# Prompt q, k and v in products of 512 columns, with one buffer for evictions and another opening order

## The chip, the cores and the metric

The kernel runs on one core of a Trainium2 chip. The core's engines run side by side and wait for each other through semaphores: TensorE (PE in the profile, with the loads of its stationary operand as PEld), VectorE (DVE), ScalarE (ACT), GpSimd (POOL) and SyncE (SP), which here issues nearly all transfers, in the order of its own queue. The metric is the device time of one execution in microseconds (us), median of several runs.

## The reference, cut to what matters

One encoder layer is applied to a prompt of 1024 tokens and to a sample of 512 tokens, with a model width of 1024. Everything is float32.

```python
def encoder_layer(x, ...):
    h = rmsnorm(x, norm_g)
    z = h @ w_in
    hy_in, hy_gate, att_qkv, att_gate = jnp.split(z, [3*HY_W, 4*HY_W, 4*HY_W + 3*ATT_W], axis=-1)
    ...                                  # Hyena branch: short and long convolution
    q, k, v = jnp.split(att_qkv, 3, axis=-1)                 # 512 columns each, 8 heads of 64
    q = rmsnorm(q.reshape(B, L, N_HEADS, HEAD_DIM), qn_g)
    k = rmsnorm(k.reshape(B, L, N_HEADS, HEAD_DIM), kn_g)
    y_att = neighbourhood_attention(q, k, v, rpb)
    y_att = rmsnorm(y_att, on_att) * jax.nn.silu(att_gate)
    return x + jnp.concatenate([y_hy, y_att], axis=-1) @ w_out
```

The Hyena branch's filter is a small network (mlp) of sines on positions, with two layers and a third product w3, multiplied by a decay; its spectrum K is multiplied with that of the branch's input.

## The kernel before

A float32 product is made of three products of a high and a low part: hi x whi, hi x wlo, lo x whi. The parts of the normalised, transposed input are hThi_p and hTlo_p, one tile for each segment of 512 prompt tokens, with 8 pieces of 128 channels (KC = 8). A weight key is loaded by SP into wraw and split into two units, whi by a cast on ScalarE and wlo by a subtraction, mostly on GpSimd (`issue_w`); `take_w` hands the units out and keeps up to `w_bufs` = 4 of them ready.

**Opening.** `x_norm` loads and scales four x tiles of a segment, `x_turn` transposes them on TensorE (L246) and makes hThi on ScalarE and hTlo on VectorE. `mlp_seg` is one layer of the filter's mlp for 512 positions: a product (L168), steps on VectorE (arg, n: L76 to L82) and a sine on ScalarE. VectorE's order is written out by hand in `run` (manual_schedule): segment 0's x and hTlo, all of segment 1's x and hTlo, the first mlp layer, then the splitting of w3 (w3lof, w3lob) and of the transform constants (fc, dftm). Behind that a scheduler sets the order by priorities and its own estimate of times.

**First phase.** `weave` merges two chains: the filter phase (`k_phase`: products with w3 (L562, L563), a product with the decay `dec` on VectorE giving xk, sums and differences into zc and bt tiles, transforms (L453 to L455, L468) and ScalarE's copies Kw), and the projections: v, two blocks of the attention gate, then k and q. `proj_tok` makes 256 columns of v, k or q for all 1024 tokens in one pass: h is stationary, the weights move, four banks of PSUM hold two token tiles of 256 columns each, and the weights of a pass (four units) are used up in it. v, k and q take two passes each, so there are six passes of 192 products of 128x256 at L414. The gates come from `proj_ch` (L401), where the weights are stationary and 512 tokens move.

**Evictions.** Each bank of v is cast into a tile `vg` (ScalarE, L855), its remainder is subtracted (VectorE, recorded at the helper's L64) and four stores of 160 KB bring vg to DRAM (v_p). A gate's SiLU (L872) goes into a tile of the same name. There are `nvg` = 2 buffers for `vg`, and as many for `qsq`, the squares of q and k. In the filter phase dec has 3 buffers, zc 4 (`nz`), bt 3 (`nb`).

## Time and profile before

| | us |
|---|---|
| median of 3 runs | 1055.24 |
| lowest and highest run | 1054.57, 1055.99 |
| profiled execution, its own time | 1052.45 |
| span of the profiled execution | 1050.7 |
| TensorE busy | 991.8 |
| VectorE busy | 777.4 |
| ScalarE busy | 454.4 |
| GpSimd busy | 395.0 |

The rows further below come from the profiled execution. Their times count from the start of its span; what its own time has beyond the span lies around it. The first v product starts at 18.93 us, the first gate product at 92.95, the first product of k at 120.49, and the first Hyena product at 269.41. An engine that is busy for most of the span need not be the one that decides in each stage, so the rows are read by stage.

### The profile page before, as it was taken

What the parts mean: (1) busy time and instruction counts of PE and PEld (TensorE: products, weight loads), DVE (VectorE), ACT (ScalarE), POOL (GpSimd) and SP (SyncE); (2) the same over time, 40 slices, a digit from 0 to 9 for tenths busy, and PEclk for the clock granted to TensorE, in tenths of its full rate; (3) what the DMA queues carried; (4) which work ended last, traced back from release to release, by engine and by line L of the source; (5) the groups of instructions that cost most, each with busy time, mean ns of one, the idle gap of its engine ahead of it and who ended that gap; (6) DMA issues with size and microseconds to landing.
All of it is one profiled execution on the core that took longest, in us unless ns stands there. A gap on an engine that the chain in (4) does not pass through costs nothing.

```text
span 1050.7 us, 16730 instructions
## 1 busy us (share of the span) xinstructions
PE 991.8 (94%) x5868; PEld 873.1 (83%) x5868; DVE 777.4 (74%) x2039; ACT 454.4 (43%) x942; POOL 395.0 (38%) x315
## 2 busy tenths in 40 slices
PE   5889999999999999999998999998999989999998
PEld 3779799899888888888887887888988877878776
DVE  4795949654368776868558999989887877757675
ACT  7333334423331323221215565565766653456441
POOL 0012212342342322424156533435354355664540
PEclk9989999999999999999999999999999999999999
DMA  7146661653422121211393333644644469644432
GB/s 290 61 157 208 212 215 56 221 182 123 134 88 83 45 68 51 88 39 68 133 300 110 110 111 107 178 130 133 195 138 128 125 215 324 171 144 129 148 108 107
DMA packets 105491, 147.95 MB, mean 141 GB/s; under 512 B 7633, under 2 KB 69915, under 8 KB 104895
## 3 DMA queue, kind: packets, MB, share of 16 engines
q1 hardware_dynamic: 105176, 146.44, 44.6%
q8 instruction: 47, 0.77, 0.3%
q10 hardware_dynamic: 231, 0.44, 0.2%
q14 instruction: 37, 0.30, 0.1%
HBM read 105.89 MB, written 40.96 MB: 140 GB/s over the span
## 4 chain that ended last, share of the span: by engine, by line
PE 60%; DVE 20%; DMA 10%; ACT 4%; issue 3%; SPq 2%; POOL 1%; DVEq 0%; ACTq 0%; POOLq 0%
PE bank L401 26%; PE bank L414 8%; PE bank L1108 8%; PE bank L453 4%; PE bank L1022 2%; PE bank L1013 2%; PE bank L454 2%; PE bank L455 2%; DVE zc L64 2%; SPq L61 2%; DVE whi L374 1%; DVE s_sb L991 1%; DMA lo<-A_p 1%; DVE bt L64 1%; DVE s L64 1%
## 5 line engine op out<-in xcount | busy, mean ns | idle before, releaser
L64 POOL TENSOR_TENSOR wlo<-wraw,whi 128x512 fp32r<-128x512 f32 x148 | 225.5, 1529 | 474.4 <-ACT whi L374 325.7
L401 PE MATMUL bank<-hThi_p,whi 128*128 128x512 f32 x320 | 126.1, 394 | 0.8 <-DVE vg L64 0.8
L401 PE MATMUL bank<-hThi_p,wlo 128*128 128x512 f32 x320 | 126.2, 394 | 0.0
L401 PE MATMUL bank<-hTlo_p,whi 128*128 128x512 f32 x320 | 125.6, 392 | 0.0
L414 PE MATMUL bank<-whi,hThi_p 128*128 128x256 f32 x384 | 111.4, 293 | 0.8 <-ACT hThi_p L248 0.8
L414 PE MATMUL bank<-wlo,hThi_p 128*128 128x256 f32 x384 | 111.5, 291 | 0.0
L414 PE MATMUL bank<-whi,hTlo_p 128*128 128x256 f32 x384 | 110.3, 291 | 0.0
L995 ACT ACTIVATE s_sb<-s_sb,mx 128x360 f32<-128x360 f32 (+1 forms) x96 | 60.4, 630 | 83.7 <-DVE mx L991 82.8
L374 ACT CAST whi<-wraw 128x512 fp32r<-128x512 f32 x66 | 40.7, 621 | 99.6 <-PE bank L401 69.7
L1108 PE MATMUL bank<-whi,hi 128*128 128x512 f32 x192 | 76.9, 402 | 1.8 <-DVE acc L76 1.1
L1108 PE MATMUL bank<-wlo,hi 128*128 128x512 f32 x192 | 77.0, 401 | 0.0
L414 PEld LDWEIGHTS bank<-whi,hThi_p 128*128 128x128 f32 x384 | 74.9, 196 | 2.2 <-ACT hThi_p L248 1.2
L414 PEld LDWEIGHTS bank<-wlo,hThi_p 128*128 128x128 f32 x384 | 75.2, 196 | 1.2 <-issue 1.0
L1108 PE MATMUL bank<-whi,lo 128*128 128x512 f32 x192 | 75.7, 399 | 0.0
L414 PEld LDWEIGHTS bank<-whi,hTlo_p 128*128 128x128 f32 x384 | 74.4, 195 | 0.5 <-issue 0.5
L401 PEld LDWEIGHTS bank<-hThi_p,whi 128*128 128x128 f32 x320 | 60.2, 188 | 12.8 <-DVE vg L64 1.2
L1022 PE MATMUL bank<-pt,V 120*64 120x256 f32 (+1 forms) x352 | 67.2, 297 | 3.2 <-DVE pt L64 2.3
L401 PEld LDWEIGHTS bank<-hTlo_p,whi 128*128 128x128 f32 x320 | 60.2, 188 | 11.9
L401 PEld LDWEIGHTS bank<-hThi_p,wlo 128*128 128x128 f32 x320 | 60.2, 188 | 11.8
L64 POOL TENSOR_TENSOR T<-cmask,qkr 128x480 f32<-128x480 f32 x32 | 39.6, 1244 | 78.8 <-DMA qkr<-in_rpb_dram 64.3
L401 PE MATMUL bank<-hThi_s,whi 128*128 128x512 f32 x160 | 64.1, 404 | 3.4 <-ACT vg L835 3.1
L401 PE MATMUL bank<-hTlo_s,whi 128*128 128x512 f32 x160 | 63.4, 400 | 0.0
(278 smaller groups left out, 2663.6 us busy)
## 6 DMA issues: line engine op xcount, KB each, us to landing
wraw<-in_w_ch_dram SPq DMA_DIRECT2D x40, 512.0 KB
wraw<-in_w_tk_dram SPq DMA_DIRECT2D x24, 512.0 KB
V<-v_p SPq DMA_DIRECT2D x32, 240.0 KB
wraw<-in_w_out_dram SPq DMA_DIRECT2D x24, 256.0 KB
out_dram<-acc SPq DMA_DIRECT2D x24, 256.0 KB
v_p<-vg SPq DMA_DIRECT2D x32, 160.0 KB
K_p<-Kw SPq DMA_DIRECT2D x4, 1088.0 KB
x<-in_x_prompt_dram SPq DMA_DIRECT2D x8, 512.0 KB
```

The lines of the kernel that those rows point to most:

```text
L61: eng.dma_start(out=out, in_=in_)
L64: (eng or self.nc.vector).tensor_tensor(out=out, in0=a, in1=b, op=op)
L374: next(self.w_round)(out=hi, in_=r)
L401: nc.tensor.matmul(ps, lhsT=w, rhs=h[s][:, k], start=(k == 0 and i == 0), stop=(k == KC - 1 and i == 2))
L414: nc.tensor.matmul(pss[t // 2][:, t % 2, :], lhsT=h[t // 4][:, k, t % 4 * P:(t % 4 + 1) * P], rhs=w, start=(k == 0 and i == 0 and t % 2 == ...
L453: mm(o, lhsT=c, rhs=z, start=True, stop=False)
L454: mm(o[:, 0:P], lhsT=ns if inverse else s, rhs=z[:, 1], start=False, stop=False)
L455: mm(o[:, P:], lhsT=s if inverse else ns, rhs=z[:, 0], start=False, stop=True)
L995: nc.scalar.activation(out=s_sb[:, :n], in_=s_sb[:, :n], func=AF.Exp, bias=mx, scale=-1.0, accum_out=l)
L1013: nc.tensor.transpose(out=tp_[0:120, c * P:(c + 1) * P], in_=s_sb[:, c * 120:(c + 1) * 120], identity=self.ident)
L1022: nc.tensor.matmul(o, lhsT=vl, rhs=pr_, start=(c == 0 and i == 0), stop=(c == ncu - 1 and i == 1))
L1108: nc.tensor.matmul(ps, lhsT=a, rhs=w, start=(k == 0 and i == 0), stop=(k == 3 and i == 2))
```

## The change

The prompt's v, k and q come from a new function, `proj_wide`: products of 512 columns, for one segment of 512 tokens (four token tiles, one PSUM bank each). Pass 0 takes eight weight units, whi and wlo, and holds them for pass 1, so the weights are still loaded once. Six passes of 96 products of 128x512 take the place of six of 192 products of 128x256. The eight held units need eight buffers: four are in a new pool `w1`, which is closed after the first phase. A wide key is loaded by two transfers of 128x2x256. v's layout in DRAM becomes one tensor for each half, with rows of all 8 heads, and its prompt stores are 40x1024.

The filter and store buffers of the first phase become fewer: `nvg` 2 to 1, zc 4 to 3, bt 3 to 1, dec 3 to 2, and the mlp's n 2 to 1. The raw tile of the sample's q and k has one buffer where it had two. The evictions of q and k move into a helper, `qk_norm`.

In the opening, VectorE's order is another: segment 1's scaling stands between the last hTlo of segment 0, the first mlp layer's steps between the hTlo of segment 1, and each segment of the second mlp layer ahead of the splits of w3, fc and dftm.

```diff
+    def proj_wide(self, G, base, s, held):
+        pss = [self.bank(next(self.mm_tags)) for _ in range(4)]
+        for k in range(KC):
+            if not s:
+                held.append(self.take_w(("w_wide", base, k // 2)))
+            whi, wlo = held[k]
+            for t in range(4):
+                for i, (w, h) in enumerate(((whi, G.hi), (wlo, G.hi), (whi, G.lo))):
+                    self.nc.tensor.matmul(pss[t], lhsT=h[s][:, k, t * P:(t + 1) * P], rhs=w,
+                                          start=(k == 0 and i == 0), stop=(k == KC - 1 and i == 2))
...
+            pool = self.w1 if key[0] == "w_wide" and key[2] % 2 else next(self.w_pools)
...
-                decs.append(fp.tile([P, 2, 256], F32, name="dec", bufs=3))
+                decs.append(fp.tile([P, 2, 256], F32, name="dec", bufs=2))
...
+            if G is self.P_:
+                held = []
+                for s in range(G.nseg):
+                    raw = self.qk_norm(tp, self.proj_wide(G, base, s, held), 1)
...
+            pss = self.proj_wide(G, 4, gi, held) if big else self.proj_tok(4 + gi, G.hi, G.lo, G.nt)
...
+                        if big:
+                            self.dma(dst[:, gi * 4 + m].rearrange("x h d -> x (h d)"), src.rearrange("p h d -> p (h d)"))
...
-            list(self.mlp_seg(Gp, mp, 0, 1))
-            list(self.mlp_seg(Gs, mp, 0, 0))
+            turn = self.x_turn(Gp, 1, hp1)
+            next(turn)
+            next(turn)
+            for G, sg in ((Gp, 1), (Gs, 0)):
+                for _ in itertools.zip_longest(self.mlp_seg(G, mp, 0, sg), itertools.islice(turn, 3)):
+                    pass
+            a = self.mlp_seg(Gp, mp, 1, 0)
+            next(a)
             self.w3_load(mp)
+            list(a)
...
-        self.nz, self.nZ, self.nb, self.nraw = 4, 3, 3, 2
-        self.nvg = 2
+        self.nz, self.nZ, self.nb, self.nraw = 3, 3, 1, 2
+        self.nvg = 1
```

Three places show how the order of instructions moves. First VectorE in the opening, before the change, from the last hTlo of segment 0 to the first of segment 1:

```order
L76 SCALAR_TENSOR_TENSOR hTlo_p_234<-bank_284,pc_70,hThi_p_233 128x512
...
L80 TENSOR_SCALAR x_293<-x_293,rs_y4_310 128x1024
L80 TENSOR_SCALAR x_297<-x_297,rs_y4_310 128x1024
L80 TENSOR_SCALAR x_301<-x_301,rs_y4_310 128x1024
L80 TENSOR_SCALAR x_305<-x_305,rs_y4_310 128x1024
L64 TENSOR_TENSOR wlo_333<-wraw_223,whi_332 128x512
L64 TENSOR_TENSOR wlo_337<-wraw_223,whi_336 128x512
L76 SCALAR_TENSOR_TENSOR hTlo_p_341<-bank_342,pc_70,hThi_p_340 128x512
```

The same place after the change:

```order
L76 SCALAR_TENSOR_TENSOR hTlo_p_235<-bank_299,pc_70,hThi_p_234 128x512
L80 TENSOR_SCALAR x_245<-x_245,rs_y4_285 128x1024
L76 SCALAR_TENSOR_TENSOR hTlo_p_235<-bank_307,pc_70,hThi_p_234 128x512
L80 TENSOR_SCALAR x_249<-x_249,rs_y4_285 128x1024
L76 SCALAR_TENSOR_TENSOR hTlo_p_235<-bank_315,pc_70,hThi_p_234 128x512
L80 TENSOR_SCALAR x_253<-x_253,rs_y4_285 128x1024
L76 SCALAR_TENSOR_TENSOR hTlo_p_235<-bank_323,pc_70,hThi_p_234 128x512
L80 TENSOR_SCALAR x_257<-x_257,rs_y4_285 128x1024
L64 TENSOR_TENSOR wlo_335<-wraw_223,whi_334 128x512
```

The root steps for segment 1 (rs_h4, rs_y4, rs_t4) stood where the dots are and now stand ahead of the piece; the four scalings moved from behind the last hTlo to between the last four.

Then SP's queue in the gate stage, before the change, where vg_1168 and vg_1175 hold the first evicted banks of the second v pass:

```order
L61 DMA dec_564<-in_dec_p_dram 128x512
L61 DMA v_p10_99<-vg_1168 40x2x512 x2
L61 DMA dec_572<-in_dec_p_dram 128x512
L61 DMA hyb_849<-in_hy_bias_dram 1x128
L61 DMA v_p11_100<-vg_1168 40x2x512
L61 DMA dec_580<-in_dec_p_dram 128x512
L61 DMA hT0_75<-px_522 128x4x128
L61 DMA dec_588<-in_dec_p_dram 128x512
L61 DMA hyb_1248<-in_hy_bias_dram 1x128
L61 DMA hT1_76<-px_522 128x4x128
L61 DMA v_p11_100<-vg_1168 40x2x512
L61 DMA v_p10_99<-vg_1175 40x2x512
```

The same place after the change, where vg_1001 and vg_1008 hold them:

```order
L61 DMA v_p0_97<-vg_1001 40x1024 x2
L61 DMA v_p1_98<-vg_1001 40x1024
L61 DMA wraw_699<-in_w_tk_dram 128x2x256
L61 DMA dec_545<-in_dec_p_dram 128x512
L61 DMA dec_547<-in_dec_p_dram 128x512
L61 DMA hyb_549<-in_hy_bias_dram 1x128
L61 DMA wraw_699<-in_w_tk_dram 128x2x256
L61 DMA wraw_734<-in_w_tk_dram 128x2x256 x2
L61 DMA dec_558<-in_dec_p_dram 128x512
L61 DMA v_p1_98<-vg_1001 40x1024
...
L61 DMA v_p0_97<-vg_1008 40x1024 x2
```

The first dec loads, which stood ahead of these stores, now stand between them, with two weight keys, and the stores of vg_1008 come a whole eviction later.

Last, ScalarE in the gate stage, before the change, from the third eviction to the gates' SiLU (bank_1307 is the first gate product's bank):

```order
L855 CAST vg_1182<-bank_954 128x8x64
L374 CAST whi_1468<-wraw_1297 128x512
L260 ACTIVATE hl_1229,pss_1228<-px_1226 128x1024
L855 CAST vg_1189<-bank_955 128x8x64
L374 CAST whi_1472<-wraw_1297 128x512
L872 ACT_TABLE_LOAD
L872 ACTIVATE vg_1357<-bank_1307 128x512
```

The same place after the change (bank_1141 is the first gate product's bank):

```order
L895 CAST vg_1015<-bank_903 128x8x64
L895 CAST vg_1022<-bank_904 128x8x64
L386 CAST whi_1487<-wraw_1300 128x512
L386 CAST whi_1491<-wraw_1300 128x512
L386 CAST whi_1303<-wraw_1130 128x512
L917 ACT_TABLE_LOAD
L917 ACTIVATE vg_1191<-bank_1141 128x512
```

The order of the evictions and the SiLU is the same, but the tiles named vg now share one buffer, and the weight casts that stand between are of other keys.

## Rows read from the trace of the kernel before

**Rows 1.** The profile's page: PE's busy time, and the chain's shares by engine.

```profile
PE 991.8 (94%) x5868; PEld 873.1 (83%) x5868; DVE 777.4 (74%) x2039; ACT 454.4 (43%) x942; POOL 395.0 (38%) x315
PE 60%; DVE 20%; DMA 10%; ACT 4%; issue 3%; SPq 2%; POOL 1%; DVEq 0%; ACTq 0%; POOLq 0%
```

**Rows 2.** Windows: length, busy time by engine, PE's clock share, DMA share, GB/s.

```profile
18.00:31.00 13.00, 10.55 (x71) 10.14 (x70) 6.47 (x11) 9.79 (x18) 0.00 (x0) 1.00 0.33 123
31.00:37.00 6.00, 3.00 (x14) 2.57 (x15) 5.62 (x17) 0.58 (x1) 0.00 (x0) 0.72 0.02 4
37.00:57.50 20.50, 20.50 (x165) 19.54 (x164) 16.11 (x31) 9.18 (x17) 3.87 (x3) 1.00 0.24 78
57.50:62.20 4.70, 0.42 (x5) 0.22 (x3) 4.64 (x9) 1.64 (x4) 1.48 (x1) 0.86 0.06 4
62.20:68.00 5.80, 5.80 (x22) 4.77 (x23) 5.65 (x15) 0.62 (x2) 0.00 (x0) 0.52 0.83 301
68.00:93.00 25.00, 24.57 (x201) 23.91 (x199) 16.15 (x30) 12.31 (x26) 4.12 (x4) 1.00 0.57 182
93.00:120.50 27.50, 26.73 (x130) 22.28 (x130) 20.91 (x53) 6.67 (x12) 3.79 (x3) 1.00 0.84 268
120.50:269.40 148.90, 143.80 (x1114) 139.24 (x1113) 93.21 (x297) 57.71 (x148) 42.86 (x29) 1.00 0.47 151
269.40:302.80 33.40, 33.40 (x150) 27.59 (x149) 13.51 (x30) 12.03 (x24) 14.93 (x13) 1.00 0.48 156
```

**Rows 3.** Waits of PE from 18 to 93 us: total, times, longest.

```profile
PE bank L246 <- DVE x L80: 4.7, 1, 4.7
PE bank L168 <- DVE arg L82: 4.3, 1, 4.3
```

**Rows 4.** Waits of PE from 121 to 303 us.

```profile
PE bank L453 <- ACT Kw L588: 3.3, 3, 1.4
PE bank L453 <- ACT Kw L594: 1.1, 1, 1.1
```

**Rows 5.** Chain of waits from 60 to 310 us: start, length, what, count.

```profile
251.18 18.23 PE bank L414 x152
269.41 33.35 PE bank L401 x147
```

**Rows 6.** The same chain, opening to gate stage: small PE work and two transfers.

```profile
23.52 0.44 PE bank L246 x4
...
69.88 0.86 PE bank L168 x2
...
86.49 5.05 DMA dec<-in_dec_p_dram
...
104.54 5.54 DMA v_p<-vg
```

**Rows 7.** Timeline of ScalarE, 54 to 126 us: start, length, instruction, wait before it.

```profile
56.84 1.06 ACT L855 CAST vg<-bank 128x512 fp32r<-128x512 f32 x2
...
70.45 0.59 ACT L855 CAST vg<-bank 128x512 fp32r<-128x512 f32 x1 [4.62 <-DMA v_p<-vg]
...
102.42 0.59 ACT L855 CAST vg<-bank 128x512 fp32r<-128x512 f32 x1 [6.36 <-DMA v_p<-vg]
...
110.12 0.59 ACT L855 CAST vg<-bank 128x512 fp32r<-128x512 f32 x1 [1.55 <-DMA v_p<-vg]
...
114.37 1.28 ACT L872 ACT_TABLE_LOAD   x1 [3.15 <-DMA v_p<-vg]
```

**Rows 8.** Timeline of VectorE: the first two v remainders.

```profile
62.03 1.27 DVE L64 TENSOR_TENSOR vg<-bank,vg 128x512 fp32r<-128x512 f32 x2
```

**Rows 9.** Timeline of SP's queue: time that issuing the v stores takes.

```profile
94.76 0.53 SPq L61 DMA_DIRECT2D v_p<-vg  x1
...
98.27 1.17 SPq L61 DMA_DIRECT2D v_p<-vg  x2
...
103.61 2.87 SPq L61 DMA_DIRECT2D v_p<-vg  x5
...
113.23 3.47 SPq L61 DMA_DIRECT2D v_p<-vg  x4
```

More of the change, by code (lines that the diff above doesn't have):

```diff
@@ L137, in setup @@
             nr = 16 if G.name == "p" else 9
-            self.v_d[G.name] = [[self.dr.tile([nr * 40, 4, P], F32, name=f"v_{G.name}{i}{hf}") for hf in range(2)] for i in range(2)]
+            self.v_d[G.name] = [self.dr.tile([nr * 40, 8, P], F32, name=f"v_{G.name}{hf}") for hf in range(2)]
     def mlp_setup(self, fl, mp):
@@ L170, in mlp_seg @@
         self.ts(arg, ps, b, ALU.add, fr, ALU.mult)
-        n = mp.tile([P, 512], F32, name="n", bufs=2)
+        n = mp.tile([P, 512], F32, name="n", bufs=1)
         magic = 12582912.0
@@ L298, in steps @@
             return [[("w_tk", 4 + gi, hf) for hf in range(2)] for gi in range(2)]
+        if what in ("qkp", "vp"):
+            return [[("w_wide", b, j) for j in range(4)] if s == 0 else [] for b in ((2, 0) if what == "qkp" else (4,)) for s in range(2)]
         if what[:2] == "ga":
@@ L343, in load_w @@
     def load_w(self, raw, key):
+        if key[0] == "w_wide":
+            _, b, j = key
+            for g in range(2):
+                self.dma(raw.rearrange("p (k g c) -> p k g c", k=2, g=2)[:, :, g],
+                         self.io["w_tk"][b + g, j // 2].rearrange("p (k c) -> p k c", k=4)[:, j % 2 * 2:j % 2 * 2 + 2])
+            return
         if key[0] != "w_out":
@@ L357, in fetch_w @@
             self.w_pos += 1
-            pool = next(self.w_pools)
-            raw = pool.tile([P, 1024], F32, name="wraw", bufs=2)
+            pool = self.w1 if key[0] == "w_wide" and key[2] % 2 else next(self.w_pools)
+            raw = (self.wp if pool is self.w1 else pool).tile([P, 1024], F32, name="wraw", bufs=2)
             self.load_w(raw, key)
@@ new lines, in qk_proj @@
+            if G is self.P_:
+                held = []
+                for s in range(G.nseg):
+                    raw = self.qk_norm(tp, self.proj_wide(G, base, s, held), 1)
+                    for gi in range(2):
+                        self.dma(self.qk_d[G.name][nm, gi].rearrange("(t p) c -> p t c", p=P)[:, s * 4:(s + 1) * 4],
+                                 raw[:, :, gi * 256:(gi + 1) * 256])
+                    yield
+                continue
+            for gi in range(2):
+                raw = self.qk_norm(tp, self.proj_tok(base + gi, G.hi, G.lo, G.nt), 2)
@@ L843, in qk_proj, with qk_norm @@
                 self.dma(self.qk_d[G.name][nm, gi].rearrange("(t p) c -> p t c", p=P), raw)
                 yield
+    def qk_norm(self, tp, pss, n):
+        nc = self.nc
+        C = 512 // n
+        nb = len(pss)
+        raw = tp.tile([P, nb * n, C], F32, name="raw", bufs=1 if n == 1 else 1)
+        ss = tp.tile([P, nb * 8], F32, name="qss", bufs=2)
+        flat = raw.rearrange("p t c -> p (t c)")
+        for m, ps in enumerate(pss):
+            nc.scalar.copy(out=flat[:, m * 512:(m + 1) * 512], in_=ps)
+            sq = tp.tile([P, 512], F32, name="qsq" if n == 1 else "vg", bufs=self.nvg)
+            nc.scalar.activation(out=sq, in_=ps, func=AF.Square)
+            nc.vector.tensor_reduce(out=ss[:, m * 8:(m + 1) * 8], in_=sq.rearrange("p (h d) -> p h d", d=HD), axis=AX.X, op=ALU.add)
+        r = self.rsqrt(tp, ss, nb * 8, 1.0 / HD, "q")
+        rv = flat.rearrange("p (h d) -> p h d", d=HD)
+        for m in range(nb):
+            o = rv[:, m * 8:(m + 1) * 8]
+            self.mul(o, o, r[:, m * 8:(m + 1) * 8].rearrange("p (n o) -> p n o", o=1).broadcast_to([P, 8, HD]), nc.gpsimd)
+        return raw
@@ L845, in v_proj @@
     def v_proj(self, G, tp):
         nc = self.nc
-        nt = G.nt
+        big = G is self.P_
+        held = []
         for gi in range(2):
-            pss = self.proj_tok(4 + gi, G.hi, G.lo, nt)
+            pss = self.proj_wide(G, 4, gi, held) if big else self.proj_tok(4 + gi, G.hi, G.lo, G.nt)
             for m, ps in enumerate(pss):
-                vh = tp.tile([P, 2, 4, P], F32R, name="vg", bufs=self.nvg)
-                pv = ps.rearrange("p t (h d) -> p (t h) d", d=HD)
-                vf = vh.rearrange("p t h d -> p (t h) d")
-                nc.scalar.copy(out=vf[:, :, 0:HD], in_=pv)
-                self.sub(vf[:, :, HD:P], pv, f32(vf[:, :, 0:HD]))
+                vh = tp.tile([P, 8, P], F32R, name="vg", bufs=self.nvg)
+                pv = (ps if big else ps.rearrange("p t c -> p (t c)")).rearrange("p (h d) -> p h d", d=HD)
+                nc.scalar.copy(out=vh[:, :, 0:HD], in_=pv)
+                self.sub(vh[:, :, HD:P], pv, f32(vh[:, :, 0:HD]))
@@ L865, in v_proj @@
                 for hf in range(2):
[L866 removed]
+                    self.dma(self.v_d[G.name][hf][320:360, gi * 4:(gi + 1) * 4].rearrange("x h d -> x (h d)"), zt)
             yield
@@ L956, in load_head @@
             for hf in range(2):
-                vd = self.v_d[G.name][h // 4][hf][:, h % 4, :]
+                vd = self.v_d[G.name][hf][:, h, :]
                 if big:
```

66 lines of the change are left out of this document (34 added, 32 removed).

## The prediction

> **What bounds the kernel now.** I read the page first: TensorE (PE) is busy 94% of the span and holds most of the chain that ended last, VectorE (DVE) 20% of it and transfers 10% [rows 1]. So a change that spares PE time is worth something only where PE is not waiting for the others. The table of windows says where that is [rows 2]. Between 18 and 93 us, the v stage, PE is idle in three places and its clock falls behind two of them (0.72 in 31:37, 0.52 in 62.2:68). In the gate stage (93 to 120.5) it is idle 0.8 us. From 120.5 to 269.4, the q and k stage, it is idle 5.1 us in 149, and in the first Hyena products behind that not at all. The waits of PE name what ended the idle time: the scaling of x and the mlp's arg, both on VectorE [rows 3], and later the filter transform's Kw copies on ScalarE [rows 4].
>
> **The wide products.** The chain has two undisturbed stretches: 152 products of 256 columns in 18.23 us, 119.9 ns each, and 147 of 512 columns (proj_ch, the same engine and the same type) in 33.35 us, 226.9 ns each [rows 5]. Two narrow ones become one wide one, so each wide product saves 2 x 119.9 - 226.9 = 12.9 ns. There are 1152 narrow products, 576 wide ones: 192 for v save 2.5 us, 384 for q and k save 5.0 us. The rows can be read as a price per product, whatever its width, of about 13 ns above the columns. The Trainium skill ("TensorE: Matmul & The Clock Gate", Back-to-back issue gap) gives the isolated gap as the columns over 2.4 plus about 2.5 ns; by it the saving would be 576 x 2.5 = 1.4 us and not 7.4 (an estimate from that page). The rows of this trace disagree with it, and I take the rows.
>
> **The opening and the v stage.** Work of PE between the first product and the first gate product, after the change: 192 x 0.2269 = 43.6 us, 13 groups of four transposes at 0.44 = 5.7, four mlp products at 0.86 = 3.4 [rows 6], and about 2.4 us of filter products and transposes of the sample. That is 55.1 us; before, the same with 384 x 0.1199 is 57.6 us, and the stage lasts 74 us, so 16.4 us are idle time (10.2 us by the windows) and low clock. The new VectorE order leaves the first wait (4.7 us for x) about where it is: the second segment's scaling still stands behind the same transposes and root steps. The second wait, 4.3 us for arg behind w3lo and fc, goes, since the mlp's steps now stand ahead of those loads; with it goes the low clock of 62.2:68 (2.8 us). Pass one then ends at 18.9 + 96 x 0.2269 + 5.7 + 2.6 + 4.7 + 1 = 54.7 us, and the first v bank is evicted at about 54.5, behind w3lo.
>
> **The v evictions, the term that decides.** A v bank is freed by a cast (ScalarE, 0.59) and a subtraction (VectorE, 0.64 each) into a vg buffer [rows 7, 8]; four stores then empty the buffer. Before there are two vg buffers, and ScalarE still waits for stores: 4.62 us at 70.45, 6.36 at 102.42, 3.15 at 114.37 [rows 7]. After the change there is one buffer, so eight evictions and the first gate's SiLU stand in one line, and each costs c = cast and subtraction 1.4, the issue of three more stores at 0.6 to 0.87 each [rows 9] about 2.2, and the landing of the last one. The chain has a landing of 5.54 us with up to eight stores of both buffers and the dec loads about [rows 6] at a DMA share of 0.84 [rows 2]; with one buffer and two dec buffers fewer are in flight, and I take 4.4. So c = 8.0. Below, 3.5 for the landing gives 7.1. Above, the order puts the last store of vg_1001 behind two weight loads and dec loads that wait for VectorE, and those of vg_1008 behind two dec loads and px; before, such a place cost a gap from the store at 94.76 to the one at 98.27 [rows 9], 3.5 us. With it in three evictions of eight and a landing of 5.05 to 5.54, c is 9.5. The value 8.0 lies nearest to the uncrowded sum, as five of the eight evictions are.
>
> The first q or k product needs the bank of the first gate, whose SiLU needs the buffer: 54.5 + 8c + 0.5 us (SiLU and its table load 1.28, less the next cast and subtraction), with c = 8.0 about 119.0 against 120.5 before [rows 2]. By PE's own work it could start at 54.7 + 25.0 (what pass two leaves of the 55.1) + 27.7 (the gate stage's 26.7 and two filter products and transposes more) = 107.4. So of the 2.5 us of rate and the waits and low clock removed, all but **1.5 us** are given back in the line of evictions. Each microsecond on c is 8 us of time.
>
> **q and k.** Rate: **5.0 us**, in a stage where PE is busy 97%. Waits there: 5.1 us before, 4.4 of it for Kw [rows 4]. The order now puts the filter products of the second pair behind 84 wide products where 72 narrow ones stood (19.1 us against 8.6), and the last block's transforms within the first Hyena products, so PE reaches each later; I take half of the waits away, **2.5 us** (bounds 0 and 5). Against it: the second gate's SiLU now waits for the first's store, 512 KB in the one buffer, **-2.0** (0 to -4); eight held weight units change over together between k and q, **-1.0** (0 to -3): ScalarE's casts and GpSimd's subtractions for them are as many as before, but come together. Fewer buffers of zc, bt and dec: **-0.5** (0 to -4), as VectorE and the transfers take turns more strictly. Each wide weight key is two loads of half the size: 24 more issues on SP's queue at about 0.45 us, 11 us over 200 us of a queue that mostly waits, and the data come as before a pass early; at nothing, up to 1 us if not. One raw buffer for the sample's q and k, one n buffer in the mlp and the larger rows of the v stores: nothing; the n buffer's cover is that the mlp's steps follow one another on VectorE anyway. Stages behind 303 us are written out as before and only shift in the scheduler's order: nothing, ±4.
>
> **Sum.** 1.5 + 5.0 + 2.5 - 2.0 - 1.0 - 0.5 = 5.5 us. The profiled execution took 1052.45 us (span 1050.7), so 1046.9 would be its answer; it lies 2.8 us below the median of the three runs, 1055.24, so the median becomes **1049.7 us**.
>
> **The rivals.**
> 1. *The line of evictions is longer (slower).* One vg buffer, in the gate stage: stores on SP behind dec loads that wait for VectorE, whose xk products wait for a dec load that was itself queued behind a store. For it: the 6.36 us wait with two buffers, and the rows of SP's order. Against: five of eight evictions have no dec load among their stores. At c = 8.7 the gain is used up; at 9.2 the time is 1059.3 us.
> 2. *The evictions run smoothly (faster still).* With c = 7.1 the first q product comes at 111.8, still behind PE's own work, and the sum is 12.7 us: 1042.5 us. For it: the stores are rows of 4 KB now and fewer transfers share the queues. Against: the landing rows are 5 us and more.
> 3. *The filter phase is the bound until 227 us.* The chain from 86 to 227 us goes through dec loads, VectorE and Kw [rows 4, 6]. Then the 5.0 and the 2.5 are turned into waits, and two dec buffers lengthen the chain: about 1056 us. Against: PE waits for it only 5.1 us now, and its steps stand later in PE's order.
> 4. *The wide form brings little.* The narrow token products and the wide channel products differ in more than width: which operand is stationary. If a wide token product takes twice a narrow one, 239.8 ns, the 7.4 us are missing; those of v are hidden by the evictions, so 5.0 us: 1054.7 us. The gap in the Trainium skill's page leans this way. Against: the 226.9 ns stand in rows of this kernel, with a stationary tile of the same shape.
>
> **How the numbers follow.** My forecast (c between 7.5 and 8.4, 1045 to 1053 us) has 0.36, the smooth evictions 0.23, the long ones 0.19, the filter bound 0.17, the small gain per product 0.05. A measurement of this kernel can tell 0.2%, 2.1 us. Faster by more (below 1053.1): 0.36 + 0.23 = 0.59 with none of the others. Same (1053.1 to 1057.4): rivals 3 and 4, 0.22. Slower: rival 1, 0.19. The range runs from c = 7.0 (1041) to rival 1 at c = 9.1 (1058.5, rounded to 1059); outside I leave 1 in 10 on either side.
>
> **What would show it.** Right: matmuls of 512 columns 226.9 ns apart in q and k; no wait for arg; casts of vg 7.5 to 8.5 us apart from 54 to 117 us, each waiting for stores; first q or k product at 116 to 122 us; PE idle under 4 us from there on. Wrong: casts over 9 us apart with idle PE in the gate stage (rival 1), PE waiting over 8 us for xk, zc or Kw between 120 and 270 us (rival 3), or a cadence near 240 ns (rival 4). A shift of more than 4 us behind 303 us would be a cause that I have not priced.

## The result: 2.5% slower, and the profile after

| | before | after |
|---|---|---|
| median, us | 1054.9 (4 runs) | 1079.36 (4 runs, 1078.25 to 1080.44) |
| ratio, 95% interval | | 1.0254 (1.0227 to 1.0281) |
| span of the profiled execution, us | 1050.7 | 1077.6 |

I had forecast 1049.7 us in a range of 1041 to 1059. The change costs 24 us where I expected a gain of 5.5. The page of the changed kernel shows a PE with fewer instructions (5292 for 5868) that is busy longer than before [rows 1]:

```profile
PE 999.0 (93%) x5292; PEld 847.4 (79%) x5292; DVE 799.8 (74%) x2039; ACT 454.9 (42%) x940; POOL 385.3 (36%) x315
```

The windows say where the time went. I cut both traces at the same events: v, gate (before: 93.0 to 120.5), k and q, first Hyena products up to the first Hyena transposes, attention up to the output projection. For the kernel before, the gate stage and k and q stand in [rows 2]; these are its last two stages, with the columns of [rows 2]:

```profile
269.40:302.60 33.20, 33.20 (x149) 27.39 (x148) 13.51 (x30) 11.83 (x24) 14.77 (x12) 1.00 0.48 157
547.50:856.10 308.60, 292.16 (x1815) 260.69 (x1815) 271.55 (x689) 189.16 (x388) 139.51 (x113) 0.98 0.47 136
```

And the five of the changed kernel:

```profile
19.00:90.80 71.80, 63.69 (x273) 48.55 (x273) 53.01 (x102) 30.38 (x57) 6.78 (x6) 0.93 0.34 111
90.80:133.30 42.50, 34.42 (x137) 27.43 (x138) 28.47 (x60) 12.67 (x24) 14.04 (x10) 0.84 0.68 211
133.30:267.50 134.20, 131.21 (x673) 112.00 (x672) 95.82 (x263) 51.29 (x127) 34.28 (x25) 0.99 0.47 152
267.50:318.20 50.70, 40.56 (x183) 33.32 (x182) 26.06 (x62) 15.17 (x35) 12.58 (x10) 0.90 0.41 137
565.50:882.50 317.00, 295.70 (x1832) 262.31 (x1832) 268.09 (x689) 187.75 (x385) 137.26 (x112) 0.98 0.45 133
```

Stage by stage: v 2.2 us shorter, gate 15.0 longer (42.5 for 27.5), k and q 14.7 shorter [rows 2], first Hyena products 17.5 longer, the stage between these and attention 2.4 longer (247.3 for 244.9), attention 8.4 longer, and what follows it 0.5 longer. The attention stage lies far behind the first phase, and PE's busy time in it differs by 3.5 us only (295.7 for 292.2). The first product of k comes 12.8 us late (133.3 for 120.5) and the first Hyena transposes come 15.6 us late (318.2 for 302.6).

The cadence of the wide products is as forecast. In a run of products without others between, the starts lie 0.23 us apart (timeline of PE: start, length, instruction):

```profile
212.58 0.40 PE L440 MATMUL bank<-wlo,hThi_p 128*128 128x512 f32 x1
212.81 0.40 PE L440 MATMUL bank<-whi,hTlo_p 128*128 128x512 f32 x1
213.05 0.39 PE L440 MATMUL bank<-whi,hThi_p 128*128 128x512 f32 x1
213.28 0.39 PE L440 MATMUL bank<-wlo,hThi_p 128*128 128x512 f32 x1
```

The evictions stand in one line, and their period is longer than forecast (timeline of ScalarE, the columns of [rows 7]):

```profile
58.43 0.59 ACT L895 CAST vg<-bank 128x512 fp32r<-128x512 f32 x1 [3.28 <-PE bank L440]
...
66.95 0.59 ACT L895 CAST vg<-bank 128x512 fp32r<-128x512 f32 x1 [6.10 <-DMA v_p<-vg]
...
74.17 0.59 ACT L895 CAST vg<-bank 128x512 fp32r<-128x512 f32 x1 [2.88 <-DMA v_p<-vg]
...
80.81 0.59 ACT L895 CAST vg<-bank 128x512 fp32r<-128x512 f32 x1 [1.95 <-DMA v_p<-vg]
...
89.40 0.59 ACT L895 CAST vg<-bank 128x512 fp32r<-128x512 f32 x1 [1.25 <-DMA v_p<-vg]
...
102.40 0.59 ACT L895 CAST vg<-bank 128x512 fp32r<-128x512 f32 x1 [0.23 <-DMA v_p<-vg]
...
113.98 0.59 ACT L895 CAST vg<-bank 128x512 fp32r<-128x512 f32 x1 [0.38 <-DMA wraw<-in_w_tk_dram]
...
123.27 0.59 ACT L895 CAST vg<-bank 128x512 fp32r<-128x512 f32 x1 [8.70 <-DMA v_p<-vg]
...
130.26 1.28 ACT L917 ACT_TABLE_LOAD   x1 [2.14 <-DMA v_p<-vg]
```

The eight periods from 58.43 to 130.26 are 9.0 us each in the mean (6.6 to 13.0), not 8.0, and the line starts 3.9 us later than I had put it (58.4 for 54.5). The first product of k comes at 133.3, not at 119.

The stage with the largest loss, the first Hyena products, has one long wait of PE, 7.8 us for cx, a step of the Hyena convolution on VectorE. Three timelines show what it waits for, ScalarE's Kw copies of the filter phase, SP's queue, then VectorE:

```profile
297.17 0.77 ACT L614 ACTIVATE Kw<-bank 64x256 f32<-64x256 f32 x2 [11.71 <-DMA K_s<-Kw]
```

```profile
288.93 1.14 SPq L61 DMA_DIRECT2D K_s<-Kw  x1
...
300.69 0.32 SPq L61 DMA_DIRECT2D K_s<-Kw  x1
301.10 0.38 SPq L61 DMA_DIRECT2D o<-in_hmat_dram  x1
```

```profile
299.23 0.17 DVE L617 MEMSET Kw<- 1x128 f32 x1 [9.85 <-ACT Kw L616]
...
304.77 0.43 DVE L64 TENSOR_TENSOR dftm<-o 128x256 f32<-128x256 f32 x1 [5.10 <-DMA o<-in_hmat_dram]
305.49 0.43 DVE L64 TENSOR_TENSOR dftm<-s 128x256 f32<-128x256 f32 x1 [0.29 <-DMA s<-in_hmat_dram]
305.83 1.40 DVE L76 SCALAR_TENSOR_TENSOR cx<-bank,pc,cx 128x512 f32<-128x512 f32 x2
```

```profile
308.28 0.79 PE L413 MATMUL bank<-hThi_p,whi 128*128 128x512 f32 x1 [7.80 <-DVE cx L76]
```

The filter phase's last blocks run here. Kw has one buffer and waits for the store of the block ahead; VectorE stands idle 9.85 us for that Kw; the store of the last block stands on SP ahead of Hyena's transform constants, and VectorE works on these ahead of cx. PE has Hyena products up to 300.5 us and nothing else behind them, so the end of the chain stands in the open. PE's granted clock is down when it goes on (0.72 in this stretch):

```profile
300.00:318.20 18.20, 10.40 (x37) 8.08 (x36) 7.46 (x14) 6.09 (x14) 5.16 (x4) 0.72 0.54 188
```

Before, the last Kw copy was through at 251.2 us, with 18 us of token products still to come.

### The profile page after: what moved, and what is told of

It reads as the page before. It is cut to its first block, busy times and chain, and to the rows that moved or that the text cites. A ratio compares the mean times of both kernels' runs of the same rounds, so it can differ in the third digit from the quotient of the medians.

```text
span 1077.6 us, 15609 instructions
## 1 busy us (share of the span) xinstructions
PE 999.0 (93%) x5292; PEld 847.4 (79%) x5292; DVE 799.8 (74%) x2039; ACT 454.9 (42%) x940; POOL 385.3 (36%) x315
## 5 line engine op out<-in xcount | busy, mean ns | idle before, releaser
L64 POOL TENSOR_TENSOR wlo<-wraw,whi 128x512 fp32r<-128x512 f32 x148 | 206.7, 1404 | 515.8 <-ACT whi L386 360.1
L413 PE MATMUL bank<-hThi_p,whi 128*128 128x512 f32 x320 | 130.1, 407 | 12.7 <-DVE cx L76 7.8
L413 PE MATMUL bank<-hTlo_p,whi 128*128 128x512 f32 x320 | 128.7, 402 | 0.0
L413 PE MATMUL bank<-hThi_p,wlo 128*128 128x512 f32 x320 | 128.4, 401 | 0.0
L440 PE MATMUL bank<-whi,hThi_p 128*128 128x512 f32 x192 | 77.6, 410 | 2.3 <-DVE vg L64 1.5
L440 PE MATMUL bank<-wlo,hThi_p 128*128 128x512 f32 x192 | 78.2, 407 | 0.8 <-DVE wlo L64 0.8
L440 PE MATMUL bank<-whi,hTlo_p 128*128 128x512 f32 x192 | 76.0, 403 | 0.0
L426 PE MATMUL bank<-whi,hThi_s 128*128 128x256 f32 x192 | 56.8, 296 | 7.8 <-DVE cx L76 4.0
L413 PE MATMUL bank<-hThi_s,wlo 128*128 128x512 f32 x160 | 63.7, 398 | 0.0
L64 DVE TENSOR_TENSOR pt<-bank,pt 120x384 fp32r<-120x384 f32 (+1 forms) x96 | 56.3, 595 | 4.5 <-ACT pt L1060 3.7
```

What stands on the lines that cost most here:

```text
L64: (eng or self.nc.vector).tensor_tensor(out=out, in0=a, in1=b, op=op)
L413: nc.tensor.matmul(ps, lhsT=w, rhs=h[s][:, k], start=(k == 0 and i == 0), stop=(k == KC - 1 and i == 2))
L426: nc.tensor.matmul(pss[t // 2][:, t % 2, :], lhsT=h[t // 4][:, k, t % 4 * P:(t % 4 + 1) * P], rhs=w, start=(k == 0 and i == 0 and t % 2 == ...
L440: self.nc.tensor.matmul(pss[t], lhsT=h[s][:, k, t * P:(t + 1) * P], rhs=w, start=(k == 0 and i == 0), stop=(k == KC - 1 and i == 2))
```

## The experiments

All ratios are to the kernel before, on the same chip. The table puts the traces of all runs beside each other; its times come from one profiled execution each, the ratios from all executions. The filter chain is counted from the first xk to the last Kw copy of the filter phase; the last column is when the first Hyena transposes start (us).

| run | ratio (95% interval) | filter chain | length | first k product | last token product | Hyena transposes |
|---|---|---|---|---|---|---|
| before | 1 | 91.6 to 251.2 | 160 | 120.5 | 269.1 | 302.6 |
| after | 1.0254 (1.0227 to 1.0281) | 98.2 to 300.3 | 202 | 133.3 | 267.5 | 318.2 |
| e1_vg1 | 1.0041 (1.0019 to 1.0063) | 93.0 to 246.7 | 154 | 133.7 | 269.9 | 303.6 |
| e2_kbuf | 1.0024 (1.0001 to 1.0047) | 90.6 to 266.0 | 175 | 122.9 | 270.1 | 303.6 |
| e3_open | 0.9939 (0.9919 to 0.9960) | 88.3 to 251.4 | 163 | 112.5 | 267.9 | 301.3 |
| e4_narrow | 1.0057 (1.0034 to 1.0080) | 91.9 to 269.1 | 177 | 129.6 | 277.7 | 311.4 |
| e5_reload_all | 1.0143 (1.0114 to 1.0172) | 100.9 to 289.5 | 189 | 119.8 | 270.7 | 311.6 |
| e6_reload_kbuf | 1.0193 (1.0152 to 1.0233) | 100.2 to 292.2 | 192 | 134.0 | 288.3 | 323.6 |
| e7_reload_vg | 1.0171 (1.0139 to 1.0204) | 100.1 to 299.9 | 200 | 120.0 | 258.9 | 315.7 |
| e8_reload_few | 1.0318 (1.0279 to 1.0358) | 99.6 to 308.5 | 209 | 131.5 | 275.0 | 326.3 |
| e9_after_lo_act | 1.0193 (1.0159 to 1.0227) | 92.5 to 291.1 | 199 | 126.8 | 261.7 | 309.5 |
| e10_before_lo_act | 0.9970 (0.9949 to 0.9992) | 88.2 to 248.0 | 160 | 112.5 | 263.9 | 297.4 |
| e11_qk_wide | 1.0106 (1.0069 to 1.0142) | 87.2 to 284.2 | 197 | 110.8 | 279.7 | 314.0 |
| e12_v_wide | 1.0065 (1.0043 to 1.0086) | 101.5 to 264.9 | 163 | 119.5 | 276.0 | 309.5 |
| e13_split | 1.0127 (1.0107 to 1.0147) | 91.4 to 274.1 | 183 | 130.9 | 285.6 | 319.3 |

**First, the parts alone.** My first theory was that the buffers given up were the cost: the single vg buffer (V) or the filter buffers (K). The rival (W): the wide products themselves.

The single vg buffer, in the kernel before:

```diff
-        self.nvg = 2
+        self.nvg = 1
```

> The kernel before with one change: one buffer instead of two for vg (and for the squares of q and k) in the first phase. Theory V (the single vg buffer is what cost the gate stage its 11 us): the casts of vg come 8 to 13 us apart, the first product of k starts 8 to 12 us later than 120.5, and the kernel is 6 to 12 us slower than before. Theory K (the loss comes from the fewer filter buffers, which stretch the filter phase beyond the projections): the gate stage alone may lose time, but the filter phase ends before the Hyena products begin, the idle time is made up, and the kernel is within 3 us of before.

The gate stage is 7.5 us longer and the first product of k 13 us later, as in the changed kernel. But the first Hyena transposes come only 1 us later. The windows show where the loss is made up: PE does 29 instructions more in the gate stage and 36 fewer in k and q than before, and the 5.1 us of idle time in k and q are gone [rows 2] (gate stage; k and q):

```profile
98.70:133.70 35.00, 31.57 (x159) 26.58 (x158) 29.13 (x87) 12.03 (x26) 5.30 (x4) 1.00 0.58 194
133.70:270.20 136.50, 136.50 (x1078) 133.97 (x1077) 81.89 (x257) 53.69 (x134) 36.35 (x28) 1.00 0.49 165
```

So V's mechanism is there and its price isn't: 0.4%, some 4 us, which lies between the bands of the two theories, and in the trace only 1 us of it stands ahead of the Hyena transposes. The filter chain is as early as ever (93.0 to 246.7); that this is why the delay can be made up is my reading.

The few filter buffers, in the kernel before:

```diff
-                decs.append(fp.tile([P, 2, 256], F32, name="dec", bufs=3))
+                decs.append(fp.tile([P, 2, 256], F32, name="dec", bufs=2))
...
-        self.nz, self.nZ, self.nb, self.nraw = 4, 3, 3, 2
+        self.nz, self.nZ, self.nb, self.nraw = 3, 3, 1, 2
```

> The kernel before with fewer filter buffers: zc 3 instead of 4, bt 1 instead of 3, dec 2 instead of 3; vg keeps two. Theory K: the filter phase's last transform, at 250 us before, moves 10 to 30 us later, the first Hyena transposes with it, and the kernel is 6 to 15 us slower. Theory V: the filter phase is a little longer but ends within the projections; the gate stage is as before, 27 to 29 us, and the kernel is within 3 us of before.

The filter chain is 16 us longer and still ends (266) ahead of the last token product (270). So the Hyena transposes move by 1 us, and the price is 0.2%, within V's band. K's step (the chain stretches) is right, its consequence is not there as long as the products cover the chain.

The new opening alone, with x_norm and x_turn as generators, in the kernel before:

```diff
-            self.x_norm(Gp, 1, xp)
+            norm = self.x_norm(Gp, 1, xp)
+            next(norm)
             self.mlp_load(Gs)
+            list(itertools.islice(turn, 3))
+            for _ in itertools.zip_longest(norm, turn):
+                pass
...
+            a = self.mlp_seg(Gp, mp, 1, 0)
+            next(a)
             self.w3_load(mp)
+            list(a)
```

> The kernel before with the new VectorE order of the opening alone. My prediction took the wait for arg (4.3 us) and the low clock behind it (2.8 us) as gained: then the first gate product starts 5 to 7 us earlier than 92.95 and the kernel is 3 to 7 us faster. The rival, that the waits only move (to hTlo, to the second layer's weights w2, to the v evictions): first gate product within 2 us of 92.95, kernel within 2 us of before.

0.6% faster, the best kernel of the study, and faster than both that were given. The first gate product starts 5.5 us earlier and the first product of k 8.0 us earlier; at the first Hyena transposes 1.3 us of it are left in the trace. The span of this trace is only 1.7 us shorter than before (1049.0 for 1050.7), so it doesn't show where the 0.6% of the medians is gained. The k and q stage grew from 148.6 to 155.4 us: again it takes up what the stage ahead of it gives, here the other way round.

The changed kernel with products of 256 columns:

```diff
-            if G is self.P_:
+            if False:
                 held = []
...
-        big = G is self.P_
+        big = False
...
-        self.w_bufs = 8
```

> The changed kernel with the products of 256 columns instead of 512 for the prompt's v, k and q, and four weight buffers again; everything else is as changed (one vg buffer, fewer filter buffers, new opening, v's new layout, one raw buffer for the sample). Theory V with K (the buffers cost what was lost, the wide products gain 7.4 us): slower than the changed kernel by 4 to 8 us, about 1084. Theory W (the wide products with their held weights are themselves what pushes the filter phase into the Hyena products): faster than the changed kernel by 8 to 18 us, 1061 to 1071, with no wait for cx at the first Hyena products; what is then left over before, 6 to 16 us, belongs to the buffers and to the sample's part.

1.0057 stands 2.0 points below the changed kernel, some 21 us and a little more than W's band. So theory W is right in the main thing: the buffers, the opening, v's layout and the sample's raw buffer together cost 0.6% of the 2.5, and the wide passes the rest. Its attention stage, from 556.4 to 865.1 us, is 308.7 us long as before (308.6), so the sample's one raw buffer costs nothing there. The three small parts don't add up to 0.6%: alone they are +0.41, +0.24 and -0.61. I take it that with the gate stage long and the filter chain 17 us longer at the same time, the chain (269) no longer leaves the room in which the gate stage's loss was made up; no run shows this step by itself.

**Second, wide products with buffers.** Loading the wide weights a second time instead of holding them makes room for the buffers (the pool of held units goes, so w_bufs is 4 again and dec 3):

```diff
-            if not s:
-                held.append(self.take_w(("w_wide", base, k // 2)))
-            whi, wlo = held[k]
+            whi, wlo = self.take_w(("w_wide", base, k // 2))
...
-        self.nz, self.nZ, self.nb, self.nraw = 3, 3, 1, 2
-        self.nvg = 1
+        self.nz, self.nZ, self.nb, self.nraw = 4, 3, 3, 2
+        self.nvg = 2
```

> The changed kernel with the wide weights loaded again for the second pass instead of held (no pool w1, four weight buffers, 24 more weight units through ScalarE and GpSimd), which makes room for all the buffers of before: vg 2, zc 4, bt 3, dec 3. The opening stays the new one. Theory B (the wide products are good, the buffers given up for them cost the time): about as the kernel before with the new opening, 1048, less 0 to 5 us, so 1043 to 1050; first k product near 112, filter phase ends before 262, first Hyena transposes near 297 to 302. Theory W (wide products run ahead of the filter phase by themselves): the first Hyena transposes stay later than 308 and the time above 1058.

The same with the filter buffers alone back (vg 1), then with vg alone back (zc 3, bt 1, dec 2), then with neither:

> As the run with all buffers back, but with one vg buffer: only zc 4, bt 3, dec 3 are back. If the filter buffers alone decide (theory K): the gate stage is long (first k product at 125 to 135), this is made up behind it because the filter phase ends before the projections do, and the time is 1046 to 1056. If the single vg buffer decides (theory V): above 1062.

> As the run with all buffers back, but with the few filter buffers (zc 3, bt 1, dec 2) and two vg buffers. Theory K: the first k product comes early, near 112 to 118, but the filter phase ends at 285 or later, within the first Hyena products, and the time is 1060 to 1078. Theory V: 1044 to 1056.

> As the changed kernel in all its buffers (one vg, zc 3, bt 1, dec 2), with the wide weights loaded again instead of held. It tells what holding and the second pool are worth: if nothing but buffers and width matters, within 6 us of the changed kernel, 1073 to 1085; if the turnover of eight held units between passes costs time, 10 us or more below it.

Theory B falls: with all its buffers the wide kernel is still 1.4% slower than before and 2.0 points slower than the same opening with narrow products (0.9939), and the first Hyena transposes come at 311.6, as W said. Buffers are worth something to it: e6 came out as theory V had put it and e7 as theory K had, and each group alone brings 1.25 to 1.5 points of the 1.75 between e8 and e5, so they overlap. None of e5 to e8 has a filter chain under 188 us. These four load and split 24 more weight units on ScalarE and GpSimd, so they don't price the held kernel; e8 is 0.6 points above it, so of the 2.0 points some can be the reloading. They also show that the gate stage's delay is no longer made up: one vg buffer for two moves the first product of k by 14.2 us (e5 to e6) and 11.5 us (e7 to e8), and 12.0 and 10.6 us of it arrive at the Hyena transposes. In all four the filter chain ends behind the last token product; in e1 it ended 23 us ahead of it.

The halves, v narrow and k, q wide, then the reverse, both with all buffers and weights loaded again (diff against e5):

```diff
-        big = G is self.P_
+        big = False
```

> New opening, all buffers of before, v in products of 256 columns, only k and q in products of 512 with the weights loaded again for the second pass. It parts the 19 us between the kernel with everything wide and reloaded (1066.8) and the one with the new opening alone (1048). If the wide v pass at the opening is the cause (it works on one segment only and waits for hTlo and evictions, and the filter phase starts 12 us later): 1046 to 1053. If k and q are (eight units at once for GpSimd, transforms behind wide products): 1057 to 1066.

```diff
-            if G is self.P_:
+            if False:
                 held = []
```

> The other half: new opening, all buffers, only v in products of 512 with the weights loaded again, k and q in products of 256 (their squares share the two vg buffers). If the wide v pass is the cause: first xk near 100 instead of 88, first gate product at 92 to 95, time 1056 to 1066. If k and q are: 1046 to 1053.

Both came out as the theory that blames them said, so each half has a price of its own, 1.7 and 1.3 points above the opening alone with the reloading of its weights included, and together (e5) they cost 2.0, not 3. The table shows two different mechanisms. With v wide the filter chain starts 13 us later (101.5 for 88.3) and is as long as ever (163). With k and q wide it starts as early (87.2) and is 34 us longer (197). The k and q stage of that run has 18 us of idle time, where the wide products should have made it 5 us shorter (gate stage; k and q):

```profile
86.40:110.80 24.40, 24.39 (x117) 20.53 (x117) 15.63 (x35) 6.62 (x12) 3.88 (x3) 1.00 0.82 271
110.80:280.00 169.20, 150.75 (x740) 126.19 (x739) 119.75 (x315) 65.06 (x157) 65.31 (x45) 0.94 0.49 159
```

**Third, GpSimd's bursts.** Up to the first Hyena transposes VectorE does 509 instructions before and after, and is busy 21.5 us longer for them (windows from 0 to that event, of before, of after, and of a run that follows; VectorE is the third engine):

```profile
0.00:302.60 302.60, 275.32 (x1872) 253.13 (x1873) 191.25 (x509) 122.29 (x266) 71.63 (x58) 0.98 0.51 167
```

```profile
0.00:318.20 318.20, 276.81 (x1277) 224.37 (x1278) 212.71 (x509) 122.37 (x263) 68.41 (x57) 0.94 0.49 159
```

```profile
0.00:309.50 309.50, 273.03 (x1279) 223.10 (x1280) 190.03 (x509) 137.78 (x293) 25.59 (x27) 0.96 0.50 163
```

The same rows say that PE was busy 1.5 us longer there, with some 600 instructions fewer, at a lower granted clock (0.94 for 0.98). In the timeline, VectorE's steps are long where GpSimd works through the raw tiles and three weight units in a row, and have their usual length right behind (VectorE; GpSimd):

```profile
187.21 1.51 DVE L64 TENSOR_TENSOR ogh<-xk 128x256 f32<-128x256 f32 x1
188.64 2.67 DVE L64 TENSOR_TENSOR oes<-xk 128x128 f32<-128x128 f32 x2
191.23 0.68 DVE L64 TENSOR_TENSOR s<-s 128x512 f32<-128x512 f32 x1
```

```profile
180.54 6.46 POOL L64 TENSOR_TENSOR raw<-raw,rs_y 128x512 f32<-128x512 f32 x4 [1.04 <-DVE rs_y L76]
186.97 4.20 POOL L64 TENSOR_TENSOR wlo<-wraw,whi 128x512 fp32r<-128x512 f32 x3
```

To price it, GpSimd's subtraction is left out and a copy on ScalarE takes its place, so the low part holds the whole weight; in the changed kernel and, as a control, in the kernel before:

```diff
-            self.sub(lo, r, f32(hi), next(self.w_low))
+            low = next(self.w_low)
+            if low is nc.gpsimd and self.first:
+                nc.scalar.copy(out=lo, in_=r)
+            else:
+                self.sub(lo, r, f32(hi), low)
```

> The changed kernel, with the low parts of the first phase's weights (wlo) made by a copy on ScalarE instead of a subtraction on GpSimd, so the subtraction is left out and wlo is the whole weight; the order of TensorE hardly moves. It takes GpSimd's bursts away from VectorE. Theory P (VectorE's steps of the filter phase are slowed while GpSimd runs; the wide passes ask for eight units at once): the slowed steps between 170 and 260 us (zc from bt and s at 577 ns) come back near 280, VectorE's busy time in the first phase falls by 8 to 14 us, the first Hyena transposes come 6 to 14 us earlier than 318, the time falls by as much, to 1065 to 1073. Theory R (TensorE's own order is what stretches the filter phase, each transform waits behind wide products): VectorE is faster, but the filter phase ends within 4 us of the 299 us it has now, and the time is within 5 us of 1079.

> The control: the kernel before with the same copy on ScalarE in place of GpSimd's subtraction in the first phase (left out as there). GpSimd's units are spread singly over the narrow passes, so theory P expects little, 0 to 4 us faster; if it gains as much as the changed kernel does, 6 us or more, the bursts are not what sets the two apart.

The slow steps are gone. The same two steps in the changed kernel with ScalarE's copies:

```profile
180.21 0.41 DVE L64 TENSOR_TENSOR ogh<-xk 128x256 f32<-128x256 f32 x1
180.54 0.48 DVE L64 TENSOR_TENSOR oes<-xk 128x128 f32<-128x128 f32 x2
```

VectorE is busy 190.0 us up to the Hyena transposes (the third row above), as before the change, and the kernel gains 0.6 points, the control 0.3. So the bursts are real, and they cost the changed kernel 0.6 points, as theory P said (with whatever the copies on ScalarE change besides); that this is more than GpSimd already cost before (0.3) isn't clear of the intervals. Theory R as I had put it missed: the chain ends 9 us earlier, and the gain is some 6 us where R allowed 5. But the length of the filter chain hardly moves, 199 for 202 us, and 160 for 160 in the control: it mainly starts earlier. A chain that stays as long while its slow engine becomes faster isn't set by that engine. PE is idle only 3.0 us of 134 in the k and q stage of the changed kernel, so I read it as PE reaching the transforms late, in the order that it has. The windows of the chain, of before, of after and of e9, fit that:

```profile
91.60:251.20 159.60, 153.30 (x1098) 144.12 (x1097) 114.84 (x350) 60.68 (x151) 40.75 (x27) 1.00 0.55 176
```

```profile
98.20:300.30 202.10, 190.39 (x932) 160.45 (x932) 138.47 (x365) 70.89 (x167) 51.15 (x39) 0.96 0.48 155
```

```profile
92.50:291.10 198.60, 187.19 (x929) 158.98 (x930) 122.22 (x365) 81.95 (x187) 21.14 (x18) 0.97 0.49 158
```

Of the 42.5 us by which the chain grew, 37.1 are PE at work between its ends (some of it at a lower clock) and 5.4 are PE idle; with VectorE 16 us less busy in the chain (e9), PE's idle time stays at 11.4 for 11.7. The reading is still inferred, and the next run bears on it.

**Fourth, size or structure.** What makes that order? Either the structure of the wide passes (H: held units, one segment per pass, four banks that end together) or the size of the product (R). Size alone, in the changed kernel:

```diff
-                    self.nc.tensor.matmul(pss[t], lhsT=h[s][:, k, t * P:(t + 1) * P], rhs=w,
-                                          start=(k == 0 and i == 0), stop=(k == KC - 1 and i == 2))
+                    for c in (0, 256):
+                        self.nc.tensor.matmul(pss[t][:, c:c + 256], lhsT=h[s][:, k, t * P:(t + 1) * P], rhs=w[:, c:c + 256],
+                                              start=(k == 0 and i == 0 and c == 0), stop=(k == KC - 1 and i == 2 and c == 256))
```

> The changed kernel with each wide product cut into two of 256 columns into the same bank; held weights, passes by segment, buffers, opening and transfers stay. The saving of 7.4 us is gone by the rate. In the order the last transform of the filter phase now stands at 148 us of product work out of 160, where with whole wide products it stands at 174 out of 152 and so within the Hyena products. Theory R (with wide products the scheduler places the filter phase's steps behind more product work, and that order is what costs): filter chain about 165 to 180 us long instead of 202, first Hyena transposes at 305 to 312, the attention stage back near 309 us, time 1056 to 1066, so faster by 13 to 23 us although each product is slower. Theory H (holding eight units, passes of one segment and four banks that end together are the cost): the time stays within 6 us of 1079 plus 7, that is 1079 to 1092.

Smaller products, which take 7.4 us more by their rates, make the kernel 1.27 points faster, about 13 us, at the edge of R's band. But not by R's way in all. The windows of k and q, first Hyena products and attention, and of all up to the first Hyena transposes:

```profile
130.90:285.60 154.70, 145.25 (x1102) 140.63 (x1102) 98.26 (x292) 54.71 (x137) 37.16 (x26) 0.98 0.44 148
285.60:319.30 33.70, 33.70 (x151) 27.86 (x150) 12.93 (x31) 11.76 (x24) 13.55 (x12) 1.00 0.42 139
564.20:873.70 309.50, 291.60 (x1816) 258.97 (x1814) 274.23 (x689) 188.89 (x388) 139.58 (x113) 0.98 0.46 136
```

```profile
0.00:319.30 319.30, 284.09 (x1872) 258.77 (x1873) 198.26 (x509) 123.12 (x266) 70.15 (x59) 0.96 0.47 159
```

As R said, the filter chain is shorter (183, a little over R's 165 to 180) and its tail is out of the Hyena stage, which is back at 33.7 us. What that stage gives, 17 us, the k and q stage takes: 154.7 us for 134.2, by the slower products, the work that came back and 6 us more of idle time. So the first Hyena transposes, which I had at 305 to 312, stay at 319.3. The gain that is left comes behind them: the stage between is 2.4 us shorter, the attention stage is 309.5 us long for 317.0, and the output projection and what follows some 3 us shorter. Between e4 (1.0057) and this run the structure alone differs: 0.7 points, so the structure that H blames has a price as well, 7 us, though H's band (1079 to 1092) is missed.

## Why the prediction was wrong, step by step

- **The wide products.** Right: 226.9 ns was forecast, 0.23 us is seen. The Trainium skill ("TensorE: Matmul & The Clock Gate", Back-to-back issue gap) gives some 216 ns as the isolated gap at 512 columns; the 0.23 us seen here disagree as the rows of before did, and the measurement decides. The saving is there too: up to the Hyena transposes PE is busy 276.8 us in the changed kernel and 284.1 in e13, 7.3 us less, where 7.4 were forecast. But the forecast counted 5.0 us of it as time, and it is used up there by idle time of PE (41.4 us for 35.2).
- **The opening.** Right, and larger than I let it count: alone, it gives 0.6%. In the changed kernel the first v eviction started at 58.4, 3.9 us behind my time; the segment-wise pass waits for hTlo, x and weights and works at a lower clock (0.86 from 18 to 55 us, 0.95 before).
- **The v evictions.** The mechanism was there (eight evictions and the SiLU in one line), but it was mis-sized: c was 9.0 instead of 8.0, and the first k product came at 133.3 instead of 119.0. Of these 14.3 us, 7.8 are c, 3.9 the late start, and 2.5 that the way from the SiLU's table load to the product takes longer than I had counted. How much of that counts depends on what runs beside it, which I left out when I called it the term that decides, 8 us for each microsecond. In e1 a delay of 13 us is worth 1 us at the Hyena transposes; beside wide products 12.0 of 14.2 us arrive there (e5 to e6). The runs differ in where the filter chain ends: 23 us ahead of the last token product in e1, 9 us ahead of it in e4, where all of a delay of 9 us arrives, and behind it in e5 to e8.
- **k and q, the step that failed.** I took the transforms' later place in PE's order as a gain ("so PE reaches each later; I take half of the waits away, 2.5 us") and the last block's place within the Hyena products as harmless. Both went the other way. The stage itself did become 14.7 us shorter, but what left it stood in the open behind it: the first Hyena products took 17.5 us more, for the tail of a filter chain that is 202 us long for 160 and ends at 300 and not at 251. So the two stages together took 2.8 us more, where the sum had 4.0 us less. The open tail is where the delay shows and not all that it is: in e13 the tail is covered again, and the Hyena transposes come as late (319.3), since the k and q stage takes the time. I had seen the chain from 86 to 227 us run through the filter phase and made it rival 3, at 0.17, with the wrong ending: not that it would cancel the gain, but that it would end behind the products that had hidden it. Fewer filter buffers at -0.5 (0 to -4) were sized by waits; what they do in e2 is to make the chain 16 us longer, which costs 0.2% alone, and 1.25 points beside wide products and one vg buffer (e6 to e8).
- **Stages behind 303 us.** "Nothing, ±4" was too narrow: behind the Hyena transposes the changed kernel takes 11.3 us more, 8.4 of them in the attention stage. That stage is so long in the changed kernel, in e8 (313.6) and e9 (316.7), and not in e4 to e7, e11, e12 or e13 (308.7 to 310.7), with the same code for the stage. PE's order there is another (the sample's first token product stands behind the Hyena norm). The three have the wide products, one vg buffer and few filter buffers together; with any one of these taken back (e13, e6, e7) the order and the length are the old ones. How they tip the order stays open.
- **Rivals.** Rival 1 had the sign, the place and nearly the period, but its line of evictions is only a part: in e7, with two vg buffers and the first k product at 120.0, the Hyena transposes still come at 315.7. Rival 2 (c = 7.1), rival 3 as I had ended it, and rival 4 are refuted by the rows above. Rival 3 was also summed wrongly: its terms leave 1.5 - 2.0 - 1.0 - 0.5, a loss of 2.0 us and 1057.2 us, not about 1056. And the wide keys are 12 more issues on SP (36 loads for 24), not 24; that term stood at nothing. That several delays, each hidden alone, would meet and no longer be hidden stood in none of them.

The loss of 2.5 points, as the runs part it: -0.6 for the opening; +1.2 for the buffers given up, the layout and the rest on top of it (e3 to e4); +0.7 for the structure of the wide passes (e4 to e13); +1.3 for the size of the products (e13 to after), of which the trace has some 10 us in the attention and output stages. GpSimd's bursts are within these, at 0.6, and what they cost more than before isn't clear of the intervals. From the forecast the trace differs by 32.4 us: 14.3 up to the first product of k, 6.8 from there to the Hyena transposes, and 11.3 behind them. The steps are differences of single kernels, each of which has an order of its own, so a part's price holds beside these neighbours alone.

## What to carry to other kernels

When two chains share PE, look for the chain that ends last in the stage and ask of every edit what it does to that chain's end, not to the stage's waits: a delay of the other one can be nearly free (13 us in e1, 1 us at the end of the phase) or arrive almost whole (14 us in e6, 12 us), and work that leaves a stage may come to stand where nothing hides it. Where a scheduler sets the order, a faster instruction changes the order too; print where the slow chain's last steps stand against the work that covers them, before pricing a single rate. A change of several parts should be measured part by part: here one part was worth 0.6% and the others hid it.

## What the hardware showed that I had not expected

In the rows above GpSimd's work makes VectorE's steps 3.7 and 5.5 times as long where both have two operands in SBUF: 0.41 us became 1.51 and two of 0.24 became 1.33 each, and they were back at 0.41 and 0.24 when GpSimd's subtractions had gone to ScalarE. The Trainium skill ("SBUF — State Buffer", SBUF: two separate sides) says that the two engines share a pair of ports under an exclusive lock, held for a whole instruction. The trace agrees: a delayed step takes 1.1 us longer, a little less than one GpSimd instruction (1.4 to 1.6 us in the rows above).

A store that must land before its one buffer is free also weighed more than I thought: ScalarE stood idle 11.71 us ahead of its Kw copy at 297.17, the last 8.2 of them for a K_s store of 576 KB that SP had issued at 288.93.
